# A two-layer encoder trunk: scoped pools start 32 bytes later, one MLP quarter goes up in one pass, keys and values return in pairs

## Chip, cores and metric

The kernel runs on one core of one Trainium2 chip. The metric is the device time of one execution in microseconds (us), median of three runs; lower is better. TensorE (PE) multiplies, VectorE (DVE) and ScalarE (ACT) work on tiles, SyncE (SP) issues every transfer of this kernel from one queue, in program order.

## What is computed

`reference.py`, cut to its frame: two layers over 512 tokens of width 1024, each a token mixer, a cross-attention into 256 memory tokens with 4 heads, and an MLP of width 4096, each followed by a LayerNorm over the residual. Layer 0 mixes with an mLSTM, layer 1 with causal pooling windows.

```python
def sq_relu_mlp(x, w1, b1, w2, b2):
    return jnp.square(jax.nn.relu(x @ w1 + b1)) @ w2 + b2

def reference(x, mem, ...):
    kv = (mem @ mem_w_kv).astype(jnp.float32)
    mem_k = kv[..., :D_MODEL].reshape(B, MEM_LEN, XATTN_HEADS, XATTN_HD)
    mem_v = kv[..., D_MODEL:].reshape(B, MEM_LEN, XATTN_HEADS, XATTN_HD)
    for i in range(DEPTH):
        y = mlstm_mixer(x, ...) if i % 2 == 0 else pool_mixer(x, pool_w[j], pool_scale[j])
        x = layer_norm(ALPHA * x + y, ln_g[i, 0], ln_b[i, 0])
        x = layer_norm(ALPHA * x + memory_cross_attn(x, mem_k, mem_v, xattn_wq[i], xattn_wo[i]), ...)
        x = layer_norm(ALPHA * x + sq_relu_mlp(x, mlp_w1[i], mlp_b1[i], mlp_w2[i], mlp_b2[i]), ...)
    return x
```

## The kernel before

All products are made at close to float32 accuracy from two parts: a tile `h` (rounded) and a tile `l` (what the rounding left). `mm3` issues three matmuls for one product: h by h, l by h, h by l. A weight of 128 x 1024 numbers is a **unit**: one DMA of 512 KB into a tile `raw` (three of them; the first five units go elsewhere), a copy on ACT into `wh` (five), a subtraction on DVE into `wl` (five). A unit serves 24 matmuls when it goes up through the MLP (8 slices of the width, three matmuls each), with the 512 tokens as the moving operand, or 256 of them. Four units make one half (512 columns) of a down projection, in which the hidden activations are the stationary operand and the weights move.

The residual `x` stands in four tiles of 128 tokens. An MLP's 4096 hidden columns are done in four quarters. The first three use a seven-product scheme (`up_down`): up for all 512 tokens, then products `m` and `p` of 12 matmuls for each half of their output, 168 matmuls in a quarter, whose stationary operands are splits of the activations in the pool `hid`. `gather` adds their sums into `x`. The fourth quarter is plain, and in layer 0 it is bound up with what follows: it goes up for tokens 0 to 255 (`z = 0`, eight tiles of 24 matmuls with 256 columns), down for token tiles 0 and 1, then up and down again for tokens 256 to 511. As soon as a token tile is through its LayerNorm, layer 1's pooling mixer takes it: `window` (products `pd` with a band matrix), `mix` (products `po`), a LayerNorm, transposes `tr`, and a split into `xa1`, which layer 1's queries `q` read. These steps are deferred: `defer` and `tick` put them into the instruction stream after so many microseconds of matmuls, so that they stand among the matmuls of the next stage.

During the fourth quarter of layer 0, after the first half of its fifth tile, `gather` runs, and `pool_setup` loads the band matrix, the pool scale and the pool weights `wpr` (two units, in `raw` tiles), scales them on DVE and splits them. `kv_back` loads the split keys and values of the memory (eight tiles of 512 KB, spilled to HBM during the MLP) into the pool `vkv`.

Tiles come from pools. Five are fixed (`act`, `wh`, `wl`, `raw`, `xs`, besides small ones); others are scoped: `vkv`, `t5` and `t2` while tokens are mixed, `hid`, `rawd` and `t2` during the first three quarters of an MLP. In the built program the tiles of `act`, `wh`, `wl`, `raw` and `xs` start at multiples of 64 bytes in each partition; the scoped pools begin at byte 151136, which is 32 more than a multiple of 64, and so all tiles of `hid`, `rawd`, `t2` and `t5` start at such an address. Those of `vkv` are 4128 bytes long and alternate between the two kinds.

A scheduler decides the order in which each engine's instructions stand and which buffer a tile gets; each engine then works through its own list in order.

Of the kernel before, what the change touches and what calls it, by code (L numbers as in the profile page):

```python
# [15 lines left out]
P = 128  # L16
D = 1024
S = 512
# [23 lines left out]
def trunk(ctx: ExitStack, tc: tile.TileContext, a: dict, out: bass.AP):  # L42
# [17 lines left out]
    aux_p = pool("aux", 2, space=bass.MemoryType.PSUM)  # L60

    scoped = {}

# [19 lines left out]
    def ld(dst, src):  # L83
        nc.sync.dma_start(dst, src)
# [23 lines left out]
    def t5(name, dt=F32):  # L108
        return scoped["t5"].tile([P, 1280], dt, tag="t5", name=name)

    def t2(name, n=512, dt=F32):
# [205 lines left out]
    for q in range(4):  # L317
        r = scoped["vkv"].tile([P, 2, 516], F32, tag="vkv", name=f"xr{q}")[:, :, :S]
        for z in range(2):
            k = 2 * q + z  # L320
            ld(r[:, z], a["xT"][:, k])
            h, l = x0.k(k)
            A.copy(h, r[:, z])
            V.tensor_tensor(l, r[:, z], f32(h), ALU.subtract)
        if q == 0:
            u0 = m_unit(a["w_qk"][0])
# [67 lines left out]

    vh = [scoped["vkv"].tile([P, NT, 258], F32R, tag="vkv", name=f"vh{h}") for h in range(H)]
    vl = [scoped["vkv"].tile([P, NT, 258], F32R, tag="vkv", name=f"vl{h}") for h in range(H)]
    for h in range(H):
# [125 lines left out]
    def mem_k(n):  # L523

        t = [scoped["vkv"].tile([P, 1032], F32R, tag="vkv", name=f"k{n}{p}")[:, :1024] for p in "hl"]
        for c in range(4):
# [7 lines left out]
    def mem_v():  # L534
        for mt in range(2):
            mv.append([scoped["vkv"].tile([P, 1032], F32R, tag="vkv", name=f"v{mt}{p}")[:, :1024] for p in "hl"])
        for hf in range(2):
# [41 lines left out]
    def pool_setup():  # L579
# [5 lines left out]
        for q in range(2):  # L585
            r = raw_p.tile([P, WU], F32, tag="raw", name=f"wpr{q}")
            ld(r, a["w_pool"][q])
# [50 lines left out]
    for i in range(DEPTH):  # L638
# [244 lines left out]

        def kv_back():
            kv_flat = [scoped["vkv"].tile([P, 1032], F32R, tag="vkv", name=f"kv{n}")[:, :1024] for n in range(8)]
            for n, z in enumerate(kv_flat):
                ld(f32(z), spill[n])
            mk[:] = [kv_flat[0:2], kv_flat[2:4]]
            mv[:] = [kv_flat[4:6], kv_flat[6:8]]

        for q in range(3, 4):
            n = f"{i}{q}"
            if q == 3 and i + 1 < DEPTH:
                hid = ActT(f"h{n}")
                hid.get(0)
                for z in range(2):
                    cs = slice(256 * z, 256 * z + 256)
                    for m in range(KC):
                        if z == 0 and m == 4:
                            gather()  # L900
                            hid.get(1)
                            mixer, xnew, xa = pool_setup()
                        evh(hid.k(m, cs), m, q, feat_tile(f"h{n}{z}{m}", a["w1"][i, 8 * q + m], xm, acc_p, "acc", cs), f"{n}{z}")
                    tiles = (2 * z, 2 * z + 1)
                    for hf in range(2):
                        for t in down(hid, q, hf, tiles, n):
                            mixer(t, x)
                    if z == 0:
                        kv_back()
                x = xnew  # L910
                continue
            hid = Act(f"h{n}")
            for m in range(KC):
                if m == 4:
                    gather()
                evh(hid.k(m), m, q, feat_tile(f"h{n}{m}", a["w1"][i, 8 * q + m], xm, aux_p, "aux"), n)
            for hf in range(2):
                for t in down(hid, q, hf, range(NT), n):
# [84 lines left out]
```

## Time and profile before

| | |
|---|---|
| median of three runs | 1235.81 us (1235.68 to 1236.77) |
| the profiled execution | 1233.79 us |
| its span, first to last instruction | 1232.0 us |
| PE busy | 1210.3 us (98% of the span) |
| DVE, ACT busy | 847.7 us (69%), 587.9 us (48%) |
| moved by DMA | 148.23 MB, mean 120 GB/s |
| mean granted clock of TensorE | 0.995 |

The profile is of one execution. "Busy" is the time in which an engine had at least one instruction under way; matmuls overlap each other, so PE can be busy and still not be at its fastest: the distance between the starts of two matmuls tells their pace.

### The profile page before, as it was taken

The numbers are of one execution on the slowest core, as the hardware profiler recorded it, in microseconds if no ns is written. First come the engines' busy times: TensorE is split into PE (matmuls) and PEld (weight loads), VectorE is DVE, ScalarE is ACT, GpSimd is POOL, SyncE is SP. The second block draws the span as 40 slices with busy tenths as digits, with TensorE's granted clock in tenths as the row PEclk, the third lists the DMA queues.
The fourth block names the chain that finished last, engine by engine and source line by source line (L and its number), as shares of the span: only waits on it lengthen the run. The fifth ranks groups of instructions, "written<-read, shape, count | busy, mean of one in ns | idle before, by whom it ended". The sixth has DMA issues, their size and how long they took to land.

```text
span 1232.0 us, 15932 instructions
## 1 busy us (share of the span) xinstructions
PE 1210.3 (98%) x6313; PEld 1029.1 (84%) x6313; DVE 847.7 (69%) x1168; ACT 587.9 (48%) x867; POOL 8.5 (1%) x34
## 2 busy tenths in 40 slices
PE   9999999999999999999996999999999999999997
PEld 6877889889888888888886898998898888888886
DVE  6775366485649684594797898874877549479746
ACT  7576674334423564544544454562356445453420
POOL 0000000000000000000000000000000000000000
PEclk9999999999999999999998999999999999999999
DMA  6232348533242324134128636433231521511411
GB/s 234 68 103 86 103 127 271 189 114 121 69 158 99 103 80 159 52 89 151 35 89 293 218 115 200 149 119 137 88 118 54 187 68 57 183 35 49 123 52 68
DMA packets 44090, 148.23 MB, mean 120 GB/s; under 512 B 5324, under 2 KB 5580, under 8 KB 44016
## 3 DMA queue, kind: packets, MB, share of 16 engines
q1 hardware_dynamic: 44016, 147.23, 37.5%
q8 instruction: 49, 0.80, 0.3%
q14 instruction: 25, 0.20, 0.1%
HBM read 140.91 MB, written 6.29 MB: 119 GB/s over the span
## 4 chain that ended last, share of the span: by engine, by line
PE 92%; DVE 3%; DMA 3%; ACT 1%; issue 0%; SPq 0%; DVEq 0%; ACTq 0%
PE h L188 9%; PE h L187 9%; PE h L189 9%; PE m L188 7%; PE m L189 7%; PE m L187 7%; PE ao L189 2%; PE ao L187 2%; PE ao L188 2%; PE q L188 2%; PE q L189 2%; PE q L187 2%; PE p L188 2%; PE p L189 2%; PE p L187 2%; DMA raw<-in_w 2%
## 5 line engine op out<-in xcount | busy, mean ns | idle before, releaser
L151 DVE TENSOR_TENSOR wl<-raw,wh 128x1024 fp32r<-128x1024 f32 x184 | 224.2, 1222 | 168.9 <-ACT wh L150 166.9
L150 ACT CAST wh<-raw 128x1024 fp32r<-128x1024 f32 x184 | 193.1, 1052 | 292.8 <-PE h L188 75.9
L189 PE MATMUL h<-xm00h,wl 128*128 128x256 f32 (+1 forms) x176 | 59.1, 336 | 8.4 <-DVE wl L151 8.4
L187 PE MATMUL h<-xm00h,wh 128*128 128x256 f32 (+1 forms) x176 | 59.1, 336 | 1.1 <-ACT wh L150 1.1
L187 PE MATMUL h<-xm01h,wh 128*128 128x256 f32 (+1 forms) x176 | 59.5, 338 | 0.0
L824 DVE TENSOR_TENSOR b<-b,b 128x1024 f32<-128x1024 f32 x48 | 58.6, 1221 | 0.4
L188 PE MATMUL h<-xm00l,wh 128*128 128x256 f32 (+1 forms) x176 | 58.8, 334 | 0.0
L188 PE MATMUL h<-xm01l,wh 128*128 128x256 f32 (+1 forms) x176 | 58.8, 334 | 0.0
L189 PE MATMUL h<-xm01h,wl 128*128 128x256 f32 (+1 forms) x176 | 58.7, 333 | 0.0
L187 PE MATMUL h<-xm10h,wh 128*128 128x512 f32 (+1 forms) x144 | 52.8, 367 | 0.0
L188 PE MATMUL h<-xm10l,wh 128*128 128x512 f32 (+1 forms) x144 | 52.8, 367 | 0.0
L187 PE MATMUL h<-xm11h,wh 128*128 128x512 f32 (+1 forms) x144 | 52.8, 367 | 0.0
L189 PE MATMUL h<-xm11h,wl 128*128 128x512 f32 (+1 forms) x144 | 52.6, 365 | 0.0
L188 PE MATMUL h<-xm11l,wh 128*128 128x512 f32 (+1 forms) x144 | 52.6, 365 | 0.0
L189 PE MATMUL h<-xm10h,wl 128*128 128x512 f32 (+1 forms) x144 | 52.6, 365 | 0.0
L189 PEld LDWEIGHTS h<-xm00h,wl 128*128 128x128 f32 x176 | 33.9, 193 | 11.8 <-DVE wl L151 8.6
L187 PEld LDWEIGHTS h<-xm00h,wh 128*128 128x128 f32 x176 | 33.8, 192 | 4.6 <-ACT wh L150 1.3
L188 PEld LDWEIGHTS h<-xm01l,wh 128*128 128x128 f32 x176 | 34.0, 193 | 3.1
L188 PEld LDWEIGHTS h<-xm00l,wh 128*128 128x128 f32 x176 | 33.8, 192 | 3.3
L187 PEld LDWEIGHTS h<-xm01h,wh 128*128 128x128 f32 x176 | 34.0, 193 | 3.1
L189 PEld LDWEIGHTS h<-xm01h,wl 128*128 128x128 f32 x176 | 33.9, 193 | 3.1
L796 ACT ACTIVATE r<-h,b 128x512 f32<-128x512 f32 x48 | 32.8, 684 | 0.0
(929 smaller groups left out, 3519.5 us busy)
## 6 DMA issues: line engine op xcount, KB each, us to landing
raw<-in_w SPq DMA_DIRECT2D x96, 512.0 KB, 4.0
b<-in_w SPq DMA_DIRECT2D x48, 512.0 KB, 4.3
raw<-in_w_q SPq DMA_DIRECT2D x24, 512.0 KB, 4.1
raw<-in_w_ao SPq DMA_DIRECT2D x16, 512.0 KB, 3.6
raw<-in_w_qk SPq DMA_DIRECT2D x8, 512.0 KB, 4.9
raw<-in_w_v SPq DMA_DIRECT2D x8, 512.0 KB, 4.8
raw<-in_w_o SPq DMA_DIRECT2D x8, 512.0 KB, 4.3
raw<-in_w_k SPq DMA_DIRECT2D x8, 512.0 KB, 3.6
```

Source lines behind the costliest of these rows:

```text
L150: A.copy(h, r)
L151: V.tensor_tensor(l, r, f32(h), ALU.subtract)
L187: T.matmul(out_, l[0], r[0], start=start, stop=False)
L188: T.matmul(out_, l[0], r[1], start=False, stop=False)
L189: T.matmul(out_, l[1], r[0], start=False, stop=stop)
L796: A.activation(r, ps, AF.Relu, bias=b1[:, i, 8 * q + m : 8 * q + m + 1], scale=1.0)
L824: V.tensor_tensor(d, u, v, op)
```

## The change

Three edits. A tile of 32 bytes, `pad`, is added to the pool `st`, so that the scoped pools begin at byte 151168, a multiple of 64. In layer 0's last quarter, the up projection runs once over all 512 tokens (eight tiles of 24 matmuls with 512 columns, accumulated in the PSUM pool `aux` and not `acc`), and then the two down projections follow each other. The pool weights `wpr` are loaded into tiles of `vkv` and not of `raw`, and the spilled keys and values are loaded two tiles at a time, each pair after one token tile's LayerNorm: a copy of one column of that tile into the destination (ACT) makes the transfer wait for it. (Other lines only give the `vkv` tiles one shape, by a helper `vkv`.)

```diff
+    pad = st_p.tile([P, 8], F32, tag="pad", name="pad", bufs=1)
+    nc.vector.memset(pad, 0.0)
...
+    def vkv(name, dt=F32R):
+        return scoped["vkv"].tile([P, 1032], dt, tag="vkv", name=name)
...
-            r = raw_p.tile([P, WU], F32, tag="raw", name=f"wpr{q}")
+            r = vkv(f"wpr{q}", F32)[:, :WU]
...
-        def kv_back():
-            kv_flat = [scoped["vkv"].tile([P, 1032], F32R, tag="vkv", name=f"kv{n}")[:, :1024] for n in range(8)]
-            for n, z in enumerate(kv_flat):
-                ld(f32(z), spill[n])
-            mk[:] = [kv_flat[0:2], kv_flat[2:4]]
-            mv[:] = [kv_flat[4:6], kv_flat[6:8]]
+        kv_flat = []
+
+        def kv_back(after):
+
+            for _ in range(2):
+                n = len(kv_flat)
+                kv_flat.append(vkv(f"kv{n}")[:, :1024])
+                A.copy(kv_flat[n][:, :1], after[:, :1])
+                ld(f32(kv_flat[n]), spill[n])
...
-            if q == 3 and i + 1 < DEPTH:
-                hid = ActT(f"h{n}")
-                hid.get(0)
-                for z in range(2):
-                    cs = slice(256 * z, 256 * z + 256)
-                    for m in range(KC):
-                        if z == 0 and m == 4:
-                            gather()
-                            hid.get(1)
-                            mixer, xnew, xa = pool_setup()
-                        evh(hid.k(m, cs), m, q, feat_tile(f"h{n}{z}{m}", a["w1"][i, 8 * q + m], xm, acc_p, "acc", cs), f"{n}{z}")
-                    tiles = (2 * z, 2 * z + 1)
-                    for hf in range(2):
-                        for t in down(hid, q, hf, tiles, n):
-                            mixer(t, x)
-                    if z == 0:
-                        kv_back()
-                x = xnew
-                continue
             hid = Act(f"h{n}")
             for m in range(KC):
                 if m == 4:
                     gather()
+                    if i + 1 < DEPTH:
+                        mixer, xnew, xa = pool_setup()
                 evh(hid.k(m), m, q, feat_tile(f"h{n}{m}", a["w1"][i, 8 * q + m], xm, aux_p, "aux"), n)
+            if i + 1 < DEPTH:
+                for z in range(2):
+                    for hf in range(2):
+                        for t in down(hid, q, hf, (2 * z, 2 * z + 1), n):
+                            mixer(t, x)
+                            kv_back(x[t])
+                mk[:] = [kv_flat[0:2], kv_flat[2:4]]
+                mv[:] = [kv_flat[4:6], kv_flat[6:8]]
+                x = xnew
+                continue
```

Each engine's instructions outside of layer 0's last quarter and the stage behind it stand in the same order as before (PE's list has 192 matmuls fewer, DVE's and ACT's eight splits of weights fewer, SP's eight loads fewer). Inside of it the order moves; three places follow. Lines in the changed file stand 4 to 7 further down.

SP's queue where the fourth quarter begins; `raw91` and `raw92` are the fourth and fifth unit of this quarter, `wpr` the pool weights. Before:

```order
L84 DMA raw91_5560<-in_w1 128x1024 [waits DMAHW0_49,DVE_49]
L84 DMA wpr0_5619<-in_w_pool 128x1024 [waits DMAHW1_49,DVE_49]
L84 DMA band_5615<-in_band 128x1152 [waits DMAHW4_49,DMAHW3_49,PE_49]
L84 DMA psc_5617<-in_pool_scale 128x1024
L84 DMA wpr1_5627<-in_w_pool 128x1024 [waits DMAHW2_49,DVE_49]
L84 DMA raw92_5648<-in_w1 128x1024 [waits DMAHW5_49,DVE_49]
L84 DMA kv0_5972<-spill_3524 128x1024
L84 DMA kv1_5973<-spill_3524 128x1024
```

and now:

```order
L88 DMA raw91_5562<-in_w1 128x1024 [waits DMAHW0_49,DVE_49]
L88 DMA raw92_5650<-in_w1 128x1024 [waits DMAHW1_49,DVE_49]
L88 DMA band_5615<-in_band 128x1152 [waits DMAHW4_49,DMAHW3_49,PE_49]
L88 DMA psc_5617<-in_pool_scale 128x1024
L88 DMA wpr0_5619<-in_w_pool 128x1024
L88 DMA wpr1_5627<-in_w_pool 128x1024 [waits DMAHW2_49]
L88 DMA raw93_5687<-in_w1 128x1024 [waits DVE_49]
L88 DMA raw94_5724<-in_w1 128x1024 [waits DMAHW5_49,DVE_49]
```

The fifth unit now stands ahead of the band matrix, the scale and the pool weights, the pool weights wait for no `raw` tile, and no key or value stands among them.

DVE at the same place: `wl92` is the split of the fifth unit, `xin3` the last sums of `gather`, `s` and `h030l` the evictions of the up tiles. Before:

```order
L591 TENSOR_TENSOR wpr0_5619<-wpr0_5619,psc_5617 128x2x256 [waits DMAHW6_49,DMAHW0_49]
L742 TENSOR_TENSOR s0303_5593<-r0303_5591 128x256 [waits Activation_49]
L876 TENSOR_TENSOR xin3_2118<-xin3_2118,sum0a_3825 128x512 [waits DVE_49]
L745 TENSOR_TENSOR h030l_5448<-s0303_5593,h030h_5447 128x256 [waits DVE_49,Activation_49]
L878 TENSOR_TENSOR xin3_2118<-xin3_2118,sum0a_3825 128x512
L591 TENSOR_TENSOR wpr0_5619<-wpr0_5619,psc_5617 128x2x256
L591 TENSOR_TENSOR wpr1_5627<-wpr1_5627,psc_5617 128x2x256 [waits DMAHW1_49]
L591 TENSOR_TENSOR wpr1_5627<-wpr1_5627,psc_5617 128x2x256
L594 TENSOR_TENSOR wpl0_5624<-wpr0_5619,wph0_5623 128x1024 [waits Activation_49]
L151 TENSOR_TENSOR wl92_5651<-raw92_5648,wh92_5650 128x1024 [waits DMAHW2_49]
L594 TENSOR_TENSOR wpl1_5632<-wpr1_5627,wph1_5631 128x1024 [waits Activation_49]
L151 TENSOR_TENSOR wl93_5688<-raw93_5685,wh93_5687 128x1024 [waits DMAHW4_49,PE_49,Activation_49]
```

and now:

```order
L749 TENSOR_TENSOR s031_5521<-r031_5519 128x512 [waits Activation_49]
L883 TENSOR_TENSOR xin3_2120<-xin3_2120,sum0a_3827 128x512 [waits DVE_49]
L885 TENSOR_TENSOR xin3_2120<-xin3_2120,sum0a_3827 128x512
L752 TENSOR_TENSOR h030l_5450<-s031_5521,h030h_5449 128x512 [waits DVE_49,Activation_49]
L598 TENSOR_TENSOR wpr0_5619<-wpr0_5619,psc_5617 128x2x256
L598 TENSOR_TENSOR wpr1_5627<-wpr1_5627,psc_5617 128x2x256 [waits DMAHW2_49]
L598 TENSOR_TENSOR wpr1_5627<-wpr1_5627,psc_5617 128x2x256
L601 TENSOR_TENSOR wpl0_5624<-wpr0_5619,wph0_5623 128x1024 [waits Activation_49]
L158 TENSOR_TENSOR wl92_5653<-raw92_5650,wh92_5652 128x1024 [waits DMAHW6_49]
L749 TENSOR_TENSOR s032_5558<-r032_5556 128x512 [waits Activation_49]
L601 TENSOR_TENSOR wpl1_5632<-wpr1_5627,wph1_5631 128x1024 [waits DVE_49]
L752 TENSOR_TENSOR h030l_5450<-s032_5558,h030h_5449 128x512 [waits DVE_49,Activation_49]
```

The same work stands ahead of `wl92` in both; what has moved is which up tile's eviction stands beside it (now the second and third, before the fourth).

SP where the keys and values now return, behind the first LayerNorms of token tiles; `raw108` to `raw111` are the last units of the second down projection, `raw112` and on are layer 1's query weights. Only the changed kernel has these rows:

```order
L88 DMA raw108_6191<-in_w2 128x1024 [waits DMAHW3_49,DVE_49,Activation_49]
L88 DMA kv0_5937<-spill_3526 128x1024 [waits Activation_49]
L88 DMA kv1_5940<-spill_3526 128x1024 [waits Activation_49]
L88 DMA raw109_6197<-in_w2 128x1024 [waits DMAHW4_49,DVE_49]
L88 DMA raw110_6203<-in_w2 128x1024 [waits DMAHW5_49,DVE_49]
L88 DMA raw111_6209<-in_w2 128x1024 [waits DMAHW6_49,DVE_49]
L88 DMA kv2_5980<-spill_3526 128x1024 [waits Activation_49]
L88 DMA kv3_5983<-spill_3526 128x1024 [waits Activation_49]
L88 DMA raw112_6331<-in_w_q 128x1024 [waits DMAHW1_49,DVE_49,Activation_49]
```

Before, `kv0` to `kv3` stood directly behind `raw92`, and `kv4` to `kv7` one by one among the loads up to `raw102`, without a wait for an engine's work.

## Rows read from the trace of the kernel before

**Rows 1.** The page, busy time of the engines and the chain that ended last.

```profile
PE 1210.3 (98%) x6313; PEld 1029.1 (84%) x6313; DVE 847.7 (69%) x1168; ACT 587.9 (48%) x867; POOL 8.5 (1%) x34
...
PE 92%; DVE 3%; DMA 3%; ACT 1%; issue 0%; SPq 0%; DVEq 0%; ACTq 0%
```

**Rows 2.** Stages: busy time by engine (instructions), granted clock, DMA share.

```profile
639.77:651.28 11.51, 11.51 (x97) 11.46 (x95) 9.88 (x17) 2.84 (x5) 0.00 (x0) 1.00 0.96 341
651.28:666.22 14.94, 5.44 (x26) 5.07 (x25) 10.79 (x16) 6.14 (x9) 0.00 (x0) 0.66 0.72 251
...
674.86:697.82 22.96, 22.43 (x98) 17.79 (x97) 17.67 (x24) 11.50 (x13) 0.00 (x0) 1.00 0.73 237
697.82:733.74 35.92, 35.14 (x290) 34.55 (x289) 34.38 (x65) 19.29 (x41) 0.00 (x0) 1.00 0.38 119
733.74:755.52 21.78, 21.78 (x98) 18.02 (x97) 16.65 (x22) 9.83 (x12) 0.00 (x0) 1.00 0.58 193
755.52:790.55 35.03, 34.67 (x289) 34.30 (x288) 33.51 (x62) 16.20 (x31) 0.00 (x0) 1.00 0.53 163
```

**Rows 3.** PE in time order: start, duration; [idle before, what ended it].

```profile
652.52 0.39 PE L187 MATMUL h<-xm00h,wh 128*128 128x256 f32 x1 [1.08 <-ACT wh L150]
...
661.45 0.58 PE L189 MATMUL h<-xm00h,wl 128*128 128x256 f32 x1 [8.42 <-DVE wl L151]
661.82 0.42 PE L187 MATMUL h<-xm00h,wh 128*128 128x256 f32 x1
662.04 0.41 PE L188 MATMUL h<-xm00l,wh 128*128 128x256 f32 x1
```

**Rows 4.** Chain of waits through that stretch: start, duration, what.

```profile
642.42 8.97 DMA raw<-in_w
...
659.12 1.15 DVE wpl L594
...
660.28 3.71 DMA raw<-in_w
```

**Rows 5.** SP's issues there: start, duration, how many.

```profile
642.42 0.33 SPq L84 DMA_DIRECT2D raw<-in_w  x1
642.80 2.37 SPq L84 DMA_DIRECT2D kv<-spill  x4
```

**Rows 6.** PE: the first matmuls of five runs of matmuls, and one after.

```profile
473.95 0.40 PE L187 MATMUL h<-xm00h,wh 128*128 128x512 f32 x1
...
517.51 0.39 PE L187 MATMUL m<-b1101h,a1101h 128*128 128x512 f32 x1
...
600.42 0.39 PE L187 MATMUL m<-b1102h,a1102h 128*128 128x512 f32 x1
...
639.77 0.28 PE L187 MATMUL h<-xm00h,wh 128*128 128x256 f32 x1
...
821.03 0.40 PE L187 MATMUL ov<-pt10h,kv 128*128 128x512 f32 x1
...
823.81 0.28 PE L187 MATMUL s<-kv,q11h 128*128 128x256 f32 x1
```

**Rows 7.** PE groups, 400 to 640 us: busy, mean ns of one.

```profile
L188 PE MATMUL h<-xm01l,wh 128*128 128x512 f32 x80 | 31.1, 389 | 0.0
...
L188 PE MATMUL m<-t202l,q202h 128*128 128x512 f32 x8 | 3.2, 397 | 0.0
```

**Rows 8.** DVE in order of time.

```profile
641.18 1.22 DVE L151 TENSOR_TENSOR wl<-raw,wh 128x1024 fp32r<-128x1024 f32 x1
...
657.23 1.89 DVE L591 TENSOR_TENSOR wpr<-wpr,psc 128x512 f32<-128x512 f32 x3
...
704.19 1.41 DVE L244 SCALAR_TENSOR_TENSOR xin<-xin,rr,b 128x512 f32<-128x512 f32 x2
```

**Rows 9.** ACT's shortest form in that stretch.

```profile
694.90 0.29 ACT L238 ACTIVATE rs<-mv,eps_t 128x1 f32<-128x1 f32 x1
```

**Rows 10.** The page, DMA issues: how many, KB each, median us to landing.

```profile
kv<-spill SPq DMA_DIRECT2D x8, 512.0 KB, 6.6
```

More of the change, by code (lines that the diff above doesn't have):

```diff
@@ L317, in trunk @@
     for q in range(4):
-        r = scoped["vkv"].tile([P, 2, 516], F32, tag="vkv", name=f"xr{q}")[:, :, :S]
+        r = vkv(f"xr{q}", F32)[:, : 2 * S].rearrange("p (z t) -> p z t", z=2)
         for z in range(2):
@@ L392, in scores @@
         return [fns[n] for n in order]
-    vh = [scoped["vkv"].tile([P, NT, 258], F32R, tag="vkv", name=f"vh{h}") for h in range(H)]
-    vl = [scoped["vkv"].tile([P, NT, 258], F32R, tag="vkv", name=f"vl{h}") for h in range(H)]
+    vh = [vkv(f"vh{h}")[:, : NT * 258].rearrange("p (t m) -> p t m", t=NT) for h in range(H)]
+    vl = [vkv(f"vl{h}")[:, : NT * 258].rearrange("p (t m) -> p t m", t=NT) for h in range(H)]
     for h in range(H):
@@ L523, in mem_k @@
     def mem_k(n):
-        t = [scoped["vkv"].tile([P, 1032], F32R, tag="vkv", name=f"k{n}{p}")[:, :1024] for p in "hl"]
+        t = [vkv(f"k{n}{p}")[:, :1024] for p in "hl"]
         for c in range(4):
@@ L535, in mem_v @@
         for mt in range(2):
-            mv.append([scoped["vkv"].tile([P, 1032], F32R, tag="vkv", name=f"v{mt}{p}")[:, :1024] for p in "hl"])
+            mv.append([vkv(f"v{mt}{p}")[:, :1024] for p in "hl"])
         for hf in range(2):
```

## The prediction

> **What bounds the kernel now.** The page comes first: PE is busy for 1210.3 of 1232.0 us and makes up 92% of the chain that ended last [rows 1]. What does not shorten PE's own list, quicken its matmuls or close one of its gaps is therefore worth nothing here. Three questions follow: how many matmuls go, how fast the rest follow each other, and where the 22 us stand in which PE is idle.
>
> The pace is read from the starts of matmuls. Up through the MLP 192 matmuls with 512 columns lie between 473.95 and 517.51 [rows 6], 43.56 us or 0.2269 each. A stretch of 96 up matmuls with 256 columns takes 11.51 us [rows 2], 0.1199 each; two of these cost 0.2398, which is 0.0129 more than one of 512. One kind is slower than its form would have it: 168 products of `up_down` take from 600.42 to 639.77 [rows 6], 39.35 us or 0.2342 each, 7.3 ns more than the up matmuls; the mean length of one shows the same, 397 against 389 ns [rows 7]. Both have 128x128 stationary and 128x512 moving operands. The down products of the fourth quarter, in which the activations are stationary as well but lie in `act`, run 96 in 21.78 us [rows 2], again 0.2269, so it isn't the role that slows the products. Their stationary tiles lie in `hid`, at 32 mod 64.
>
> Nearly all of PE's idle time that matters stands in the fourth quarter of layer 0, so I cut that into windows [rows 2]. It loses nothing until 651.28; then 24 matmuls take 14.94 us, of which PE is busy for 5.44, at a mean granted clock of 0.66. Then the last 72 of the first half's up matmuls pass at the usual pace, and the downs take 22.96 where the same work for tokens 256 to 511 takes 21.78. The timeline has two gaps there, 1.08 us before 652.52 behind a `wh` and 8.42 us before 661.45 behind a `wl` [rows 3]; after the long one matmuls start 0.21 to 0.22 us apart at 256 columns, the time of the 1.2 GHz level, where 0.12 is the other. The chain says what was late [rows 4]: a unit issued at 642.42 lands 8.97 us later; the next is issued only at 660.28, when the pool weights' split `wpl`, which began at 659.12, has let go of a `raw` tile. SP's row shows what shared the DMA with the first: four key tiles issued directly behind it [rows 5], at 0.96 of the engines' time in that window [rows 2]. So the fifth unit came late because two pool weights, a band and 2 MB of keys stood around it, and `wl` in DVE's order behind the scaling.
>
> **The change, part by part.** *One pass up.* Gone are 384 matmuls of 256 columns, 384 x 0.1199 = 46.04 us; 192 of 512 take their place, 43.56. Gain 2.48. The Trainium skill (TensorE: Matmul & The Clock Gate, on why the gap between matmuls is N cycles) gives a fixed part of about 2.5 ns for each matmul, by which this gain would be an estimated 0.5 us; the rows have 12.9 ns for a pair, and the sum goes by the rows. Eight units are no longer loaded and split twice, 8 x 1.22 us on DVE [rows 8] and as many copies on ACT, off the path.
>
> *The stall.* The excess in 651.28 to 666.22 is 14.94 - 24 x 0.12 = 12.06 us. It goes if the fifth unit's `wl` is there in time. After the change PE asks for it at 639.77 + 4 x 5.45 = 661.6. The unit now stands ahead of band, scale and pool weights and has no keys behind it, so even with the 8.97 of [rows 4] it lands by 651.5. Its `wl` stands behind the scaling of the pool weights on DVE; the last three scalings began at 657.23 before and took 1.89 [rows 8], then comes `wpl` with 1.15 [rows 4] and `wl` with 1.22: if none of it moved, `wl` would be there at 661.5, just in time. But the scalings stood behind evictions of up tiles that waited for the unit landed at 651.4. I estimate the pool weights' landing without the keys: units, band, scale and pool weights, 3.1 MB from 642.4 on at the 341 GB/s of the first window [rows 2], 9.1 us, so 651.5; four scalings (2.6), a copy and two splits (3.4) make 657.5, or 658 to 659 with evictions between. That is some 3 us ahead of need. I take the whole 12.06; from below, were it 3 to 5 us late, that would be lost again (rival C).
>
> *The downs of tiles 0 and 1.* Before 22.96 with units that arrived late behind the stall, 21.78 without: 1.18 gained.
>
> *The room for the mixing.* Before, a stage of up and mixing (35.92 us, DVE 34.38) lay between two downs; the second downs took 21.78 with DVE at 16.65 and gave DVE room before the next mixing (35.03, DVE 33.51) [rows 2]. Now the downs of tiles 2 and 3 carry the mixing of tiles 0 and 1: their DVE work is 34.38 less the splits and evictions of the old up stage (about 5 more than the downs have) plus the downs' LayerNorm sums, together near 36.7, in a PE time of 34.7 (21.78 + some 12.9 of mixing matmuls). DVE falls behind PE by 2 us; units split ahead (five `wl`, 5 x 24 x 0.2269 / 2 = 13.6 us of PE) cover that. A gap has a lower bound of 0 and an upper one of about 4 (2 for this stage, and as much again for a sum `xin` such as that of 704.19, 1.41 for two [rows 8], on which the deferred steps wait). I take 1.0, nearer to 0 since the cover is longer than the excess.
>
> *The keys' return.* Four pairs in place of eight tiles at once. Each pair waits on ACT for a one-column copy; the shortest such form there takes 0.29 us [rows 9], eight make 2.3 us in a stage where ACT is busy for 19.29 of 35.92 [rows 2]: hidden. The wait matters more on SP: what stands behind `kv0` is `raw109` to `raw111`, behind `kv2` it is `raw112` and on. A pair is issued just behind a LayerNorm, about 0.5 us after the first downs end for tile 0, some 8 for tile 1, and 35 and 41 for tiles 2 and 3. The loads behind have five split units ahead of them, and `raw112` needs a tile that comes free later still. A key tile lands in 6.6 us [rows 10]; the first reader of keys, `s`, stands over 50 us behind the first pair. I take 0. From above, see rival D.
>
> *The pad.* In all three quarters of both layers' MLPs 168 products stand, 1008. If the address is what slows them, 1008 x 7.35 ns = 7.41 us come back. The attention's `ov` speaks for the address too: 12 from 821.03 to 823.81 [rows 6], 0.2317 each, with the moving operand in `t5` at 32 mod 64; its 96 would give 0.46 more. Bounds 0 to 7.9, and I take 7.4, since two kinds of matmul that share nothing else are slow and none of the aligned ones is. Against it: the 256-column matmuls on scoped tiles keep the pace of 0.12.
>
> *The sum*, on the profiled execution's 1233.79 us (1.79 around its span): - 2.48 - 12.06 - 1.18 + 1.0 - 7.41 = 1211.66. The median of the runs is 2.02 above that execution; on the median it makes 1213.7.
>
> **Rivals.** *B: the pad does nothing.* The slow products would be slow for another reason: `hid` lies in a higher region than `act`, and all slow operands lie there. Moving by 32 bytes doesn't change the region. Everything else stands: 1213.7 + 7.4 = 1221.1. The Trainium skill (SBUF — State Buffer, Specifications) has lines of 16 bytes in SBUF; by that a tile at 32 mod 64 starts at a line already, and the pad would change nothing: the same 1221.1. No row here shows such a line; the 7.3 ns are measured.
>
> *C: the stall comes back smaller.* The order in which DVE now meets the fifth unit has the scalings before `wl`, as before. If band and pool weights land late (before, they took until 657), PE waits 3 to 5 us at the fifth unit, or DVE's crowding costs as much in the second downs (the gap of 8.42 also stood in the window of clock 0.66). 1217 to 1219, with B's condition 1225.
>
> *D: slower.* SP's one queue now holds a wait for an engine's work at four places. If a LayerNorm of a token tile comes late, all weights behind that pair come late. That costs PE only beyond the split units ahead; to eat the 22.1 us of gain, 5.5 us uncovered at each of the four pairs are needed, or 8 to 12 at two. The pairs stand close behind tiles whose LayerNorm is done when PE goes on, and the cover is 13.6 us; hence unlikely. At the point where each pair costs 6, 1236.
>
> *E: nothing comes of either.* Stall as before and pad without effect, 1233.
>
> **How the numbers follow.** A, the forecast, 0.54, by itself 1210.5 to 1217 (crowding 0 to 4, `ov` with or without); B 0.27, 1218 to 1224; C 0.14; D 0.03; E 0.02. The range from 1210.5 to 1224 holds A, B and the part of C with the pad's gain; what is left out is about 0.15. A measurement of this kernel tells 0.2% (2.5 us) from no change: faster holds A, B, C, 0.95; slower D, 0.03; the rest 0.02.
>
> **What would show it.** Right: an up phase of 192 matmuls in 43.6 us at clock 1.00, without idle time at its fifth unit; 168 products in 38.1 us and a mean of 389 ns; `wh` and `wl` eight fewer; the end of layer 1's queries for the first tokens some 15 us (and the pad's share up to there) earlier against the start of the quarter. Wrong: products still at 397 ns (B); a gap behind `wl` in the up phase, or DVE busy all through the second downs with PE idle behind it (C); gaps of PE behind a weight's DMA that SP issued directly after a `kv` (D). Step by step, the pad's 7.4 us hangs on an inference from two kinds of rows, and is what I hold least firmly.

## The result

The changed kernel takes 1215.49 us in the median (1214.44 to 1218.03, four runs) against 1235.94 before: a ratio of 0.9836 with a 95% interval of 0.9819 to 0.9854, 20.5 us less. The forecast was 1213.7 with a range of 1210.5 to 1224.0. The time lies in it, but one of the sum's terms was far too large and another was too small; the experiments below were made for these two.

The profiled execution took 1216.41 us, its span 1214.6. The page's busy times and its chain, against [rows 1]:

```profile
PE 1202.3 (99%) x6121; PEld 1017.8 (84%) x6121; DVE 836.3 (69%) x1145; ACT 576.7 (47%) x851; POOL 8.4 (1%) x34
...
PE 96%; DMA 1%; DVE 1%; ACT 1%; issue 0%; SPq 0%; DVEq 0%; ACTq 0%
```

PE is busy 8.0 us less, and the span is 17.4 us shorter: more than half of that is idle time of PE that went. The stages of the fourth quarter by windows (busy time by engine, clock, DMA share): one pass up, the downs of tiles 0 and 1, the downs of tiles 2 and 3 with mixing, and the first stage of layer 1's queries up to the first `ov`:

```profile
640.39:683.91 43.52, 43.52 (x194) 36.04 (x192) 34.10 (x46) 19.91 (x26) 0.00 (x0) 1.00 0.62 203
683.91:705.69 21.78, 21.78 (x98) 18.04 (x97) 15.25 (x20) 9.90 (x13) 0.00 (x0) 1.00 0.39 123
705.69:739.26 33.57, 33.57 (x194) 29.18 (x193) 32.75 (x59) 13.77 (x31) 0.00 (x0) 1.00 0.55 187
739.26:804.63 65.37, 65.16 (x545) 64.73 (x544) 57.65 (x102) 35.42 (x73) 0.00 (x0) 1.00 0.59 195
```

Against [rows 2] the reader is to see three things. The up phase has 43.52 us with PE busy throughout and the clock at 1.00; its 24 matmuls at 0.66 are gone. The downs of tiles 0 and 1 take 21.78. And the third stage holds DVE 32.75 of 33.57 us and yet PE is never idle in it.

How near it was to a wait is seen at the fifth unit. DVE in order of time, and then PE (the last matmul of the fourth unit and the first of the fifth; the other two rows are the first of 168 products and the first up matmul behind them):

```profile
656.74 1.89 DVE L598 TENSOR_TENSOR wpr<-wpr,psc 128x512 f32<-128x512 f32 x3
658.55 1.23 DVE L601 TENSOR_TENSOR wpl<-wpr,wph 128x1024 fp32r<-128x1024 f32 x1
659.69 1.22 DVE L158 TENSOR_TENSOR wl<-raw,wh 128x1024 fp32r<-128x1024 f32 x1
```

```profile
661.92 0.39 PE L196 MATMUL h<-xm01h,wl 128*128 128x512 f32 x1
662.15 0.39 PE L194 MATMUL h<-xm00h,wh 128*128 128x512 f32 x1
...
601.36 0.40 PE L194 MATMUL m<-b1102h,a1102h 128*128 128x512 f32 x1
...
640.39 0.39 PE L194 MATMUL h<-xm00h,wh 128*128 128x512 f32 x1
```

The scalings, `wpl` and the fifth `wl` follow each other as in the prediction; `wl` is done at 660.91, and the unit's first matmul starts at 662.15. There is no bracket behind it: nothing was waited for. The margin is 1.2 us, and 0.5 more for `wl` itself, which only the third matmul reads.

The products take 640.39 - 601.36 = 39.03 us for 168, 0.2323 each, where [rows 6] gave 39.35. The group answering to the second of [rows 7] moved from 397 to 395 ns:

```profile
L195 PE MATMUL m<-t202l,q202h 128*128 128x512 f32 x8 | 3.2, 395 | 0.0
```

### The profile page after: what moved, and what is told of

It reads as the page before. It is cut to its first block, busy times and chain, and to the rows that moved or that the text cites. A ratio compares the mean times of both kernels' runs of the same rounds, so it can differ in the third digit from the quotient of the medians.

```text
span 1214.6 us, 15469 instructions
## 1 busy us (share of the span) xinstructions
PE 1202.3 (99%) x6121; PEld 1017.8 (84%) x6121; DVE 836.3 (69%) x1145; ACT 576.7 (47%) x851; POOL 8.4 (1%) x34
## 4 chain that ended last, share of the span: by engine, by line
PE 96%; DMA 1%; DVE 1%; ACT 1%; issue 0%; SPq 0%; DVEq 0%; ACTq 0%
PE h L195 10%; PE h L194 10%; PE h L196 10%; PE m L194 7%; PE m L195 7%; PE m L196 7%; PE ao L196 2%; PE ao L195 2%; PE ao L194 2%; PE q L194 2%; PE q L195 2%; PE q L196 2%; PE p L194 2%; PE p L195 2%; PE p L196 2%; PE v L194 1%
## 5 line engine op out<-in xcount | busy, mean ns | idle before, releaser
L158 DVE TENSOR_TENSOR wl<-raw,wh 128x1024 fp32r<-128x1024 f32 x176 | 214.0, 1221 | 168.6 <-ACT wh L157 166.5
L194 PE MATMUL h<-xm00h,wh 128*128 128x512 f32 (+1 forms) x144 | 52.8, 367 | 0.0
L194 PE MATMUL h<-xm01h,wh 128*128 128x512 f32 (+1 forms) x144 | 52.8, 367 | 0.0
L195 PE MATMUL h<-xm00l,wh 128*128 128x512 f32 (+1 forms) x144 | 52.7, 366 | 0.0
L196 PE MATMUL h<-xm01h,wl 128*128 128x512 f32 (+1 forms) x144 | 52.6, 366 | 0.0
L196 PE MATMUL h<-xm00h,wl 128*128 128x512 f32 (+1 forms) x144 | 52.6, 365 | 0.0
L195 PE MATMUL h<-xm01l,wh 128*128 128x512 f32 (+1 forms) x144 | 52.6, 365 | 0.0
L804 ACT ACTIVATE s<-r 128x512 f32<-128x512 f32 x48 | 30.4, 632 | 1.3
L195 PEld LDWEIGHTS h<-xm10l,wh 128*128 128x128 f32 x144 | 27.1, 189 | 4.4 <-DVE xm10l L204 0.2
L194 PEld LDWEIGHTS h<-xm10h,wh 128*128 128x128 f32 x144 | 27.2, 189 | 4.4
```

The source lines that it names most:

```text
L158: V.tensor_tensor(l, r, f32(h), ALU.subtract)
L194: T.matmul(out_, l[0], r[0], start=start, stop=False)
L195: T.matmul(out_, l[0], r[1], start=False, stop=False)
L196: T.matmul(out_, l[1], r[0], start=False, stop=stop)
L804: A.activation(s[m // 4][:, m % 4], r, AF.Square)
```

## Where the 17.4 us of the profiles came from

The first 15 us alone differ by up to 3.5 us between the executions profiled, so I cut the executions at the starts of the same matmuls. "start" is the first of the long row of `qk` matmuls, "three quarters" runs from the first product of layer 0's MLP to the first up matmul of its fourth quarter, "quarter" lies from its first up matmul to layer 1's first query, "queries" from there to the first `ov`, "rest" from the first product of layer 1's MLP to the end; "168" are layer 0's last products. The stretches left out (start to the first product, `ov` to layer 1's first product) differ by under 0.9 and 0.2 us. Times in us, worked out from the traces:

```
                 start  three quarters  quarter  queries  rest    168    span
before           13.89      205.18      115.75    65.51   300.14  39.35  1232.0
changed          15.53      204.15       98.87    65.37   299.07  39.03  1214.6
after_again      15.97      204.15       99.35    66.56   299.08  39.03  1216.7
pad_alone        13.89      204.15      117.38    65.11   299.08  39.03  1231.5
no_pad           17.41      205.18       98.99    66.10   300.14  39.35  1219.5
one_pass_only    16.57      205.19       98.90    67.63   300.14  39.35  1219.8
wpr_raw          16.85      204.15       99.39    67.28   299.08  39.03  1217.8
kv_once          15.56      204.15       98.93    67.46   299.08  39.03  1217.1
two_pass_both    16.09      205.18      114.76    65.77   300.15  39.35  1233.3
hid256           16.75      201.28       99.66    65.35   296.20  38.08  1211.1
hid256_again     16.13      201.28       99.22    66.11   296.21  38.08  1210.8
hid192           15.89      202.40       98.88    65.04   297.33  38.46  1211.2
```

The quarter and the queries gave 17.0 us, the products 1.03 in layer 0 and 1.1 in layer 1; the start took back 1.6. The first weight that layer 0's matmuls need landed later there; ACT's row in the changed kernel:

```profile
8.08 1.04 ACT L157 CAST wh<-raw 128x1024 fp32r<-128x1024 f32 x1 [2.41 <-DMA raw<-in_w_qk]
```

The same copy began at 7.27 before, 0.8 us sooner, with 0.94 us of waiting. The matmuls behind it ran at the 1.2 GHz level, granted clock 0.50, until 12.2 us. With and without the pad the start lies anywhere between 13.9 and 17.4. Up to there two things differ: the pad's memset, and the place of the second half of each input tile `xr`, which by the helper `vkv` starts 16 bytes sooner in all kernels with one pass and in none with two. The nine profiles with one pass have 15.5 to 17.4, the three with two passes 13.9, 13.9 and 16.1; whether that is chance or comes of the tile's shape was not tried, and I put it down to no edit. The medians of one kernel in two groups of runs differ by as much (1215.49 and 1217.42).

## Experiments: which start of `hid` makes the products slow

**The edits alone.** `pad_alone` adds the pad to the kernel before; `no_pad` takes it out of the changed one.

```diff
-    pad = st_p.tile([P, 8], F32, tag="pad", name="pad", bufs=1)
-    nc.vector.memset(pad, 0.0)
```

> The kernel before with the pad as its only edit. By what the changed kernel's trace shows (products 0.2323 us in place of 0.2342, 1008 of them): 1.9 us faster than before, about 1234.0. By the prediction's step on the pad it would be 7.4 us faster, 1228.5; by rival B nothing, 1235.9.

> The changed kernel without the pad. Two parts that add up: 1.9 us slower than with it, about 1217.4, with products back at 0.2342 and the fourth quarter as in the changed kernel (98.9 us from its first up matmul to layer 1's first query). If the pad also had a hand in the quarter, more.

Measured: `pad_alone` 1233.42 us against 1235.17 of before in the same group, 0.9991 (0.9978 to 1.0004): by the time alone not told from nothing. Its trace tells: 168 products in 39.03, 1.03 us less in layer 0's three quarters and 1.06 less in the rest, and a quarter that was 1.6 longer in the one execution profiled. `no_pad` has 1219.11, ratio 0.9876 (0.9861 to 0.9890), 1.7 us above what was expected, and its profile has the longest start of the twelve; its products are back at 39.35 and its quarter is 98.99. So neither part shows an effect on the other in the traces. By them the pad is worth 2.1 us, not 7.4.

**Two operands in one tile.** The rest was open: all slow operands lay high, all at 32 mod 64, and also at a certain distance from their partners. `bench` reads both operands from one large tile and shifts one of them. 

```diff
+CONFIGS += [(f"lls{n}", LO_S + d, LO_M, 2) for n, d in zip("abcdefgh", (0, 32, 64, 128, 160, 256, 352, 384))]
+CONFIGS += [(f"llm{n}", LO_S, LO_M + d, 2) for n, d in zip("abcdefg", (0, 32, 64, 128, 160, 256, 384))]
+CONFIGS += [(f"hls{n}", HI_S + d, LO_M, 2) for n, d in zip("abcdefg", (0, 32, 64, 128, 256, 352, 384))]
+CONFIGS += [(f"lhm{n}", LO_S, HI_M + d, 2) for n, d in zip("abcdef", (0, 32, 64, 128, 256, 384))]
+CONFIGS += [(f"hhm{n}", HI_S, HI_M + d, 2) for n, d in zip("abcd", (0, 32, 128, 256))]
```

> Nothing of the reference is computed (the output is zeros): one 224 KB-per-partition tile, zeroed, and groups of 24 matmuls of 128x128 by 128x512 in the three-matmul pattern of the products, 48 for each pair of start addresses of the stationary and the moving operand. Low is 2304 (stationary) and 67840 (moving), both 256 mod 512; high is 151296 and 184064, both 256 mod 512; offsets of 0 to 384 bytes are added to one of them. Theory 64 (a start off a multiple of 64 is slow): offsets of 32, 160 and 352 bytes pace at about 0.234 us, all others at 0.2269, low and high alike. Theory phase (the two operands' distance modulo 512 counts): all pairs without an offset at 0.2269, high ones too, and 0.232 to 0.234 with an offset of 128 or more, in either operand. Theory region (an operand above some address is slow): all low pairs at 0.2269, all with a high operand at 0.232 to 0.234 whatever the offset. If none of the pairs is slower than 0.228, the addresses are not the cause.

Groups of its lines (busy us and mean ns of one, which follows the pace within one pattern but is not the pace; `ll` is both operands low, `hl` a high stationary one, `lh` a high moving one; `s` or `m` says which is shifted, the last letter which shift):

```profile
L80 PE MATMUL llsg<-ar 128*128 128x512 f32 x48 | 11.4, 396 | 0.0
...
L80 PE MATMUL llsb<-ar 128*128 128x512 f32 x48 | 11.4, 395 | 0.0
...
L80 PE MATMUL llsd<-ar 128*128 128x512 f32 x48 | 11.3, 395 | 0.0
...
L80 PE MATMUL llmc<-ar 128*128 128x512 f32 x48 | 11.2, 392 | 0.0
...
L80 PE MATMUL llsf<-ar 128*128 128x512 f32 x48 | 11.1, 390 | 0.0
...
L80 PE MATMUL hlsa<-ar 128*128 128x512 f32 x48 | 11.1, 389 | 0.0
...
L80 PE MATMUL llma<-ar 128*128 128x512 f32 x48 | 11.1, 389 | 0.0
L80 PE MATMUL lhma<-ar 128*128 128x512 f32 x48 | 11.1, 389 | 0.0
...
L80 PE MATMUL hhmd<-ar 128*128 128x512 f32 x48 | 11.0, 389 | 0.0
```

High and low without a shift have the same 389 ns (`hlsa`, `llma`, `lhma`): the region is out. 395 stands at +32, but also at +128 (`llsd`), a multiple of 64 and of 128: theory 64 is out. 389 to 390 comes back at +256. From start to start, 48 matmuls each, the pace is 0.2269 without a shift (`llma`), 0.2332 at +32 of the stationary, 0.2325 at +128, 0.2342 at +352, 0.2277 at +256 (`llsf`; 0.2268 for the high one, `hlse`). So it repeats with 256, not with 512 as I had put it.

**Distance or own start.** `bench2` shifts both together, and adds small shifts and 256 columns:

```diff
+CONFIGS += [(f"both{n}", LO_S + d, LO_M + d, 512, 2) for n, d in zip("abcde", (0, 32, 64, 128, 160))]
+CONFIGS += [("both" + "f", LO_S + 32, LO_M + 64, 512, 2), ("both" + "g", HI_S + 96, HI_M + 96, 512, 2)]
+CONFIGS += [(f"mv{n}", LO_S, LO_M + d, 512, 2) for n, d in zip("abcdefg", (16, 32, 96, 128, 192, 224, 512))]
+CONFIGS += [(f"st{n}", LO_S + d, LO_M, 512, 2) for n, d in zip("abcdefg", (16, 32, 96, 128, 192, 224, 512))]
+CONFIGS += [(f"half{n}", LO_S + d, LO_M, 256, 4) for n, d in zip("abcd", (0, 32, 128, 192))]
```

> Nothing of the reference is computed (zeros go out). The same pattern of matmuls as in the run bench, to tell whether the distance of the two operands counts or where each of them starts. Theory distance (modulo 256): both operands shifted by the same 32, 64, 128 or 160 bytes pace at 0.2269 like the pair without a shift; stationary +32 with moving +64 at 0.233; +512 at 0.2269; +16, +96, +192 and +224 of one operand alone at 0.229 to 0.235. Theory own start (each operand wants a multiple of 256): both shifted together are as slow as one shifted alone, 0.232 to 0.235. With 256 columns the main kernels show 0.118 to 0.120 whatever the place, so +32, +128 and +192 should cost at most 0.001 there; if the extra time were fixed for a matmul it would be 0.126.

```profile
L80 PE MATMUL halfa<-ar 128*128 128x256 f32 x96 | 11.7, 283 | 0.0
L80 PE MATMUL halfc<-ar 128*128 128x256 f32 x96 | 11.6, 281 | 0.0
...
L80 PE MATMUL bothf<-ar 128*128 128x512 f32 x48 | 11.4, 395 | 0.0
...
L80 PE MATMUL stb<-ar 128*128 128x512 f32 x48 | 11.4, 395 | 0.0
...
L80 PE MATMUL mvf<-ar 128*128 128x512 f32 x48 | 11.4, 395 | 0.0
...
L80 PE MATMUL mva<-ar 128*128 128x512 f32 x48 | 11.3, 394 | 0.0
...
L80 PE MATMUL bothd<-ar 128*128 128x512 f32 x48 | 11.1, 390 | 0.0
L80 PE MATMUL bothb<-ar 128*128 128x512 f32 x48 | 11.1, 390 | 0.0
...
L80 PE MATMUL bothg<-ar 128*128 128x512 f32 x48 | 11.1, 389 | 0.0
...
L80 PE MATMUL sta<-ar 128*128 128x512 f32 x48 | 11.1, 389 | 0.0
```

Both shifted by 32 or 128 have 390 ns (`bothb`, `bothd`), by 96 in the high region 389 (`bothg`); with 32 and 64, 395 (`bothf`). It is the distance. It has a sign, too: the moving operand 16 ahead has 394 (`mva`), the stationary one 16 ahead 389 (`sta`), and 32 ahead 395, like the moving one's 224 (`mvf`), which is the same distance modulo 256. The pace from start to start by distance (moving less stationary, modulo 256), from both runs, with what the kernels' own products have beside it:

```
distance           0          16     32            64            96            128           160           192           224           240
bench, us    .2267-.2277   .2316  .2330-.2335  .2290-.2291   .2331-.2334   .2322-.2333   .2341-.2344   .2331-.2334   .2331-.2332   .2267
products     .2267 hid256                       .2289 hid192                .2323 changed  .2342 before
```

The two directions agree: moving +64 and stationary +192, the same distance, have 0.2291 and 0.2290. Low pairs shifted together by 32 to 160 keep 0.2272 to 0.2276, 0.5 to 0.9 ns above the unshifted 0.2267; that small rest I leave open. Left out are the first group behind the warm-up (`llsa`) and the last, repeated one of the second run (0.2280). With 256 columns nothing is lost: 0.1199 without a shift, 0.1178 to 0.1187 with 32, 128 or 192. The Trainium skill (SBUF — State Buffer, Specifications) speaks of lines of 16 bytes; by them alone a shift of 32 would cost nothing, and the 0.2330 to 0.2335 at that distance say otherwise.

**In the kernel.** `hid256` puts 128 bytes ahead of `hid` while an MLP runs, so that the distance to the weights is 0; `hid192` puts 64 (a tile of 16 numbers). The order of the engines' work stays, apart from one memset in each MLP.

```diff
-        enter(hid=12, rawd=6, t2=2)
+        enter(hpad=1, hid=12, rawd=6, t2=2)
+        hp = scoped["hpad"].tile([P, 32], F32, tag="hpad", name="hpad")
+        V.memset(hp, 0.0)
```

> The changed kernel with 128 bytes more ahead of the pool hid while an MLP runs, so that its tiles start at 256 mod 512 as those of act, wh and wl do; the order of all engines stays. Theory phase: products at 0.2269, 1008 x 5.4 ns = 5.4 us faster than the changed kernel, about 1210. Theory region, and theory 64: products stay at 0.232, the same time as the changed kernel, 1215.5.

> The changed kernel with hid at 256 mod 512 once more. Theory distance: 1008 x 5.5 ns = 5.5 us below the changed kernel of the same group. If the first measurement (2.8 us apart, on another chip) is the true size, part of the gain is lost in a wait behind the products.

> The changed kernel with hid 64 bytes further (151232, 192 mod 256), so that the moving operand lies 64 mod 256 behind it. Theory distance: the bench's 0.2290 to 0.2291 for a distance of 64, so 168 products in 38.5 us, 3.3 us faster than the changed kernel. Theory 64 (any multiple of 64 is alike): 0.2323, no difference. Theory region: 0.2323 too.

> The changed kernel once more, beside the others of this group on the same chip: ratio to before 0.982 to 0.985. It gives the difference to the two moves of hid without a difference of chips, and a second look at the span of the first 15 us, which lay between 13.9 and 17.4 in the profiles so far.

The last three ran on one chip: 1212.43 (0.9806, 0.9793 to 0.9820), 1213.29 (0.9817, 0.9803 to 0.9830), and 1217.42 for the changed kernel (0.9850, 0.9837 to 0.9864). The first `hid256`, on another chip, had 1212.68, where about 1210 was expected. The 168 products of `hid256_again` by a window, PE's time first, at the usual pace:

```profile
600.27:638.35 38.08, 38.08 (x170) 31.56 (x169) 36.70 (x39) 19.31 (x20) 0.00 (x0) 1.00 0.05 17
```

Three quarters and the rest together are 5.7 us shorter than in the changed kernel of that group (201.28 + 296.21 against 204.15 + 299.08), where 5.5 was expected, and the medians are 5.0 apart. `hid192` has 38.46 us, where 38.5 was expected; the two stretches are 3.5 us shorter, where 3.3 was expected, and the medians 4.1 apart. Its three kinds of matmul show how the mean comes about (mean ns of one: 394, 392, 389):

```profile
L195 PE MATMUL m<-t202l,q202h 128*128 128x512 f32 x8 | 3.2, 394 | 0.0
...
L194 PE MATMUL m<-t202h,q202h 128*128 128x512 f32 x8 | 3.1, 392 | 0.0
...
L196 PE MATMUL m<-t202h,q202l 128*128 128x512 f32 x8 | 3.1, 389 | 0.0
```

All three have the same distance, so at this distance the cost differs by the matmul's place in the pattern of three; why was not tried. Both versions beat the changed kernel; `hid256` is the fastest measured here.

## Experiments: which edit removed the stall

**Two passes, with the two other edits.** `two_pass_both` is the kernel before with the pool weights in `vkv` and the keys in pairs.

```diff
-            r = raw_p.tile([P, WU], F32, tag="raw", name=f"wpr{q}")
+            r = vkv(f"wpr{q}", F32)[:, :WU]
...
                             mixer(t, x)
-                    if z == 0:
-                        kv_back()
+                            kv_back(x[t])
```

> The kernel before with the pool weights in tiles of vkv and the keys in pairs behind the LayerNorms, but still two passes up and no pad. Theory A (the pace of 2.88 us a unit is too fast for the chain of band, pool weights, their scaling and the fifth unit's split on DVE): the fifth unit is needed at 4 x 2.88 = 11.5 us into the quarter and is split at about 18 to 20, so a wait of 6 to 8 us stays of the 9.5; 4 to 6 us faster than before, 1229 to 1232. Theory B (raw tiles and keys were the whole of the stall): the first 96 and next 24 matmuls run without a wait, 12 us faster, 1223 to 1224.

1233.60, ratio 0.9976 (0.9965 to 0.9987): 2.2 us below the kernel before in the same group. PE's gaps in the first half's up phase, and DVE ahead of the last of them:

```profile
656.04 0.58 PE L190 MATMUL h<-xm00h,wh 128*128 128x256 f32 x1 [2.40 <-ACT wh L153]
...
657.36 0.58 PE L190 MATMUL h<-xm00h,wh 128*128 128x256 f32 x1 [0.52 <-ACT wh L153]
...
662.81 0.58 PE L192 MATMUL h<-xm00h,wl 128*128 128x256 f32 x1 [4.65 <-DVE wl L154]
...
657.99 2.49 DVE L594 TENSOR_TENSOR wpr<-wpr,psc 128x512 f32<-128x512 f32 x4
660.40 1.22 DVE L597 TENSOR_TENSOR wpl<-wpr,wph 128x1024 fp32r<-128x1024 f32 x1
661.53 1.22 DVE L154 TENSOR_TENSOR wl<-raw,wh 128x1024 fp32r<-128x1024 f32 x1
```

Raw tiles and keys are out of the way, and still PE waits. The scheduler has here put the first two matmuls of the sixth and of the seventh unit ahead of the fifth unit's third; PE waits 2.40 and 0.52 for the `wh` of these two, and then 4.65 for the fifth unit's `wl`, which stands behind the four scalings and `wpl`. Together that is 7.6, inside theory A's 6 to 8. The gain isn't its 4 to 6, though: 9.5 less 7.6 is 1.9, and the up phase is 1.7 shorter (35.09 to 33.41). The stall itself varies by half of that: with the old order, `pad_alone` waited 10.4.

**One pass, with the other edits taken back.** `wpr_raw` loads the pool weights into `raw` again, `kv_once` issues the keys without a LayerNorm's wait, `one_pass_only` does both and has no pad. The first change below is that of `wpr_raw`, the others that of `kv_once`.

```diff
-            r = vkv(f"wpr{q}", F32)[:, :WU]
+            r = raw_p.tile([P, WU], F32, tag="raw", name=f"wpr{q}")
...
-            for _ in range(2):
+            for _ in range(8):
...
-                A.copy(kv_flat[n][:, :1], after[:, :1])
...
-                            kv_back(x[t])
+                    if z == 0:
+                        kv_back(None)
```

> The changed kernel with the pool weights loaded into tiles of raw again, so that the fifth unit is issued behind the second pool weight and the sixth waits for the first one's split, as before. Theory A (one pass alone gives enough time: a unit lasts 5.44 us and not 2.88): the up phase stays at 43.5 us or gains a wait of at most 2; 1215.5 to 1217.5. Theory B (the held raw tiles were the cause of the stall): a wait of 4 us or more behind the fifth or sixth unit, 1219 or more.

> The changed kernel with all eight tiles of keys and values issued as soon as there is a free tile, without the wait for the LayerNorms; in SP's queue six stand between the seventh and the eighth unit of the up phase. Theory A (the keys are hidden in one pass): the 3 MB delay the eighth unit by about 9 us, which the units ahead cover; 1215.5, within 1 us. Theory B (the keys in the queue were what starved PE): a wait of 3 us or more for the eighth unit or the first units of the downs, 1218.5 or more.

> The kernel before with the one pass up as its only edit: no pad, pool weights in tiles of raw, all keys issued at once. Theory A (the pace of the pass was the cause of the stall): up in 43.5 to 45.5 us, the quarter in 99 to 101 us in place of 115.75, and 1219 to 1223. Theory B (each of the three edits carries a part of it, and the run with raw tiles alone and the run with keys alone were saved by the other): the sixth unit, issued behind seven keys and the first pool weight's split, comes 3 us or more late, 1223 to 1227, with the clock lowered there.

Up phases of 43.52, 43.52 and 43.55 us, quarters of 99.39, 98.93 and 98.90: no stall in any. `one_pass_only` by windows (up; both downs; queries):

```profile
642.33:685.88 43.55, 43.55 (x193) 36.06 (x192) 33.75 (x45) 19.79 (x26) 0.00 (x0) 1.00 0.83 299
685.88:741.23 55.35, 55.35 (x289) 47.23 (x288) 48.12 (x78) 23.31 (x38) 0.00 (x0) 1.00 0.41 124
741.23:808.86 67.63, 65.39 (x545) 64.74 (x544) 57.82 (x102) 35.37 (x69) 0.00 (x0) 1.00 0.51 156
```

Seven tiles of keys and values and two pool weights stand among its units (DMA share 0.83 in the up phase), and PE runs through. A unit that lasts 5.44 us of PE in place of 2.88 gives the chain on DVE the time it needs, whatever tiles it uses. The end of the fifth unit's split `wl`, counted from the quarter's first up matmul, shows it: 21.6 us before, 21.0 in `two_pass_both`, 20.5 in the changed kernel, and 19.0, 20.8 and 19.6 in `wpr_raw`, `kv_once` and `one_pass_only`. It moves by 2.6 us at most; what moves is when PE asks for it, 11.8 us into the quarter with two passes and 22.2 with one. So theory A holds: the one pass removes the stall, and neither other edit is needed for that.

The times, though, are 1220.42 (0.9877, 0.9861 to 0.9894), 1218.79 (0.9857, 0.9843 to 0.9872) and 1221.48 (0.9881, 0.9868 to 0.9895), which misses theory A's figure for the first two by 2 to 3 us. In the table the queries take 67.3 to 67.6 in these three, 65.0 to 66.6 in the six others that run one pass, and 65.1 to 65.8 with two passes. In `wpr_raw` a chain can be read across three engines (ACT, then DVE, then PE). The last three rows are the same chain in `after_again`, the changed kernel itself:

```profile
757.27 1.05 ACT L157 CAST wh<-raw 128x1024 fp32r<-128x1024 f32 x1 [2.82 <-DMA raw<-in_w_q]
...
758.81 0.16 DVE L247 RECIPROCAL rr<-rs 128x1 f32<-128x1 f32 x1 [1.77 <-ACT rs L245]
...
761.47 0.39 PE L196 MATMUL po<-wph,d1l 128*128 128x256 f32 x1 [1.07 <-DVE d1l L204]
...
756.48 1.05 ACT L157 CAST wh<-raw 128x1024 fp32r<-128x1024 f32 x1 [2.42 <-DMA raw<-in_w_q]
...
758.03 0.17 DVE L247 RECIPROCAL rr<-rs 128x1 f32<-128x1 f32 x1 [1.42 <-ACT rs L245]
...
760.69 0.51 PE L196 MATMUL po<-wph,d1l 128*128 128x256 f32 x2 [1.06 <-DVE d1l L204]
```

ACT's copy of a query weight waited 2.82 us for its DMA. Behind it in ACT's order stands `rs`, a step of a LayerNorm; DVE waited 1.77 for that, its `d1l` came late, and PE waited 1.07. In the first profile of the changed kernel the same copy waited 0.60 and PE had no such wait, but in the second the copy waited 2.42 and PE 1.06. So the chain comes and goes from one execution to the next, and it is no cost of the pool weights' tiles.

PE's waits of 0.1 us and more in the queries add up to 1.9 us in `wpr_raw` and to 2.2 in `kv_once` and `one_pass_only`, against 0 to 1.2 in the six. The latter two have in common 1.1 to 1.2 for a `d1h`, where the six have 0.2 at most, and 0.8 for a weight's `wl`, where the six have none. So with one pass the keys in pairs are likely worth 1 to 2 us, one stage later than where they were put; for the place of the pool weights none is shown. Why the query weights' splits come later without the pairs was not tried, and what sets `wpr_raw` 3.0 us above the nearer of the changed kernel's two medians stays open.

## Why the prediction came out as it did

- **One pass up, the stall and the first downs.** Right: 35.09 + 23.02 (the second half's 192 at 0.1199) became 43.52, 14.6 us less, against 2.48 + 12.06 forecast; the downs gave 1.18 as forecast. The margin was 1.2 us and not 3, since the last three scalings began 16.4 us into the quarter, 1.1 earlier than before [rows 8] and not 2.5 to 3.5. Evictions of up tiles still stood ahead of them, and DVE waited 2.07 us for one of these, whose `r` stood on ACT behind the copy of the sixth unit:

```profile
652.66 1.05 ACT L157 CAST wh<-raw 128x1024 fp32r<-128x1024 f32 x1 [5.28 <-DMA raw<-in_w]
...
654.33 0.69 DVE L749 TENSOR_TENSOR s<-r 128x512 f32<-128x512 f32 x1 [2.07 <-ACT r L747]
```

  The cause was put half wrong. I named raw tiles and keys first; by `one_pass_only` and `two_pass_both` it is the time a unit lasts.
- **The room for the mixing.** A loss of 1.0 was taken; measured is a gain of 1.1: the mixing's share of PE was 35.92 - 23.02 = 12.9 before and 33.57 - 21.78 = 11.8 now. The term that was wrong is DVE's work, 32.75 us in 33.57 where I had 36.7 in 34.7: it did not fall behind PE. Of the gain, 0.8 is time in which PE stood idle in the old stage (35.14 busy of 35.92). Rival C didn't come; gaps of 0.2 to 1.1 us do appear in this stage and the next, at other places in each execution.
- **The keys' return.** Right as to the cost: pairs go out at 705.72 and 713.02 with the weights behind them, and PE waits for none of these:

```profile
705.72 0.80 SPq L88 DMA_DIRECT2D kv<-spill  x2
707.82 3.26 SPq L88 DMA_DIRECT2D raw<-in_w  x3
713.02 0.80 SPq L88 DMA_DIRECT2D kv<-spill  x2
717.75 13.19 SPq L88 DMA_DIRECT2D raw<-in_w_q  x3
```

  Rival D didn't come either. Taken at nothing, the pairs are likely worth 1 to 2 us in the queries once there is one pass; against the kernel before, whose queries take 65.51, that is no gain (65.37).
- **The pad.** The term that failed: 7.4 us forecast, 2.1 measured. The step that failed was to take "32 mod 64" for the reason because it was what the slow rows had in common. The products had a distance off 0 in common too, 160 modulo 256; the pad made it 128, which is still slow. The sign that I gave for being right, 168 products in 38.1 us, came with `hid256` (38.08) and not with the pad (39.03). `ov` stayed at 0.2317 (12 in 2.78 us), so the 0.46 us that I had at the upper bound did not come: its operands lie in `t5` and `vkv`, both scoped, so by the layout the pad moved the two together and left their distance (not tried on its own). The 256-column matmuls, which I held against the term, show no such cost at any distance tried. Rival B's figure for the pad, nothing, was nearer than mine (2.1 off against 5.3), but its reason is out: the region plays no part.
- **The sum.** Too high by 5.3 for the pad, too low by 2.3 for the quarter and the queries; the start's 1.6 I can't tie to an edit. On the profiled executions 1211.66 was forecast and 1216.41 came, 4.8 apart. That the medians came within 1.8 us is in part luck: the misses went opposite ways, and the changed kernel's profile lies 0.9 above its median.

## What to carry to other kernels

When a chain of loads, scalings and splits is late for one pass, look at how long one weight lasts on PE before moving tiles about: doubling that closed a wait of 9.5 us that shorter queues alone left at 7.6. Where matmuls with 512 columns pace unlike their neighbours, tabulate the two operands' distance and not each one's address, and shift one of them by a few bytes; here that was worth 5 us for 128 bytes. And cut executions at the same instructions before comparing them, and profile the same kernel twice before reading a chain as an edit's cost: here the first 15 us moved by up to 3.5 us, and a chain that looked like the price of an edit stood in the unedited kernel too.

## What was not expected of the hardware

A matmul of 128x128 by 128x512 in this three-matmul pattern takes 0.2267 to 0.2277 us when the moving operand's start less the stationary one's is 0 modulo 256 bytes, and up to 0.2344 when it isn't; with a distance of 240 it was 0.2267, with 16 0.2316. Matmuls with 256 columns show none of this, and run at 0.1178 to 0.1187 where the distance is not 0 against 0.1199 where it is.
